# Products of 64 weight columns into two halves of PSUM, and copies of 128x1024, in a batched 64x64 matmul

## The chip, the cores and the metric

The kernel runs on one core of one Trainium2 chip. The metric is the time of one execution in microseconds on the device. Three runs of the kernel before took 133.44, 133.45 and 133.59 us, a median of 133.45. All profile lines come from one profiled execution, which is longer than its span, the stretch from the first to the last recorded event.

## The reference

There are 1024 pairs of 64x64 matrices in fp32, and each pair is multiplied:

```python
"a": np.random.randn(1024, 64, 64).astype(np.float32)
"b": np.random.randn(1024, 64, 64).astype(np.float32)
return np.matmul(a, b).astype(np.float32)
```

Each of a, b and the output is 16.78 MB, so 50.33 MB cross the HBM interface. The kernel multiplies in bf16 and accumulates in fp32.

## The kernel before, in words

The batch is cut into 16 tiles of 64 matrices (n_t, index t) for b and the output, and into 8 pairs of tiles (n_s, index s) for a. The order of work is written out by hand at the end of the function, under manual_schedule(): every engine and every DMA queue takes its instructions in the order of the calls there.

**Loads.** cast_load_a() (L73) loads three quarters of a pair's a through POOL's queue and casts to bf16 on the way; load_a() (L81) loads the last quarter as fp32 through SP's queue, into a_raw. load_first_a() (L94) loads pair 0 as fp32 into two buffers borrowed from the output pool. load_b() (L100) loads one tile of b, in turn through SP's and ACT's queues, three tiles ahead.

**Making the weights.** The contraction index is split in two (u), and two bf16 values share one fp32 word. For pairs 1 to 3 (ON_DVE), transpose_dve() transposes blocks on VectorE (L131), and ScalarE casts a_raw for it (L129). For the other pairs regroup() (L109, L112, L115) sorts the rows, and transpose() transposes on TensorE (L141) and copies the result with ScalarE (L144). spread() copies the transposed a into one of two block-diagonal weight tiles at_bd (L157 and L167, on VectorE). Four matrices (h) share the 128 rows of one weight block. cast() casts b to bf16 (L176; for the last tile L181 and L183).

**Products.** multiply(t) runs, for a tile, 16 groups g of four matrices. For every g it makes four products: two values of j, and two of u that accumulate in PSUM. Each product (L221) loads 128 weight columns and streams 64 columns of b. The 128 weight columns are wl (2) by h by mp by vo, so that wl decides the half of the 128 PSUM partitions on which a result lies. A PSUM tile o_ps holds half a tile (8 groups), 128 partitions by 1024 fp32 values, and there are two of them.

**Copies out of PSUM.** evacuate() (L209) sorts a PSUM tile into the output tile o_sb. In PSUM the partitions go by wl and the parity of g lies along the row; in o_sb the partitions go by parity and wl lies along the row. So each half needs four copies of 64 partitions by 512 values. ScalarE does them, except that VectorE does two of four in the second half of the odd tiles from 7 to 13. In the last tile the PSUM tiles are quarters, borrowed from the transposes' pool (at_ps), and two quarters are copied by ScalarE, two by VectorE, four copies of 64x256 each.

**Stores.** store(t) issues the store (L198) of a tile one iteration after it is computed (HOLD = 2), on POOL's queue as one 1 MB DMA, for tile 14 as two, and for the last tile as four on SP's and ACT's queues.

**What orders the work around the change.** In iteration t come spread(t + 1) and cast(t + 1), the loads, perhaps TensorE transposes, multiply(t) with its copies, then the preparation of later pairs, then store(t - 1). spread(t + 1) writes the weight tile that multiply(t - 1) read. ScalarE's queue holds the copies of L209, the copies of L144, the casts of L129 and half of b's loads, all in that order.

Of the kernel before, what the change touches and what calls it, by code (L numbers as in the profile page):

```python
# [8 lines left out]
fp32 = mybir.dt.float32  # L9
bf16 = mybir.dt.bfloat16  # L10
# [3 lines left out]
def kernel(  # L14
# [14 lines left out]
    nc = tc.nc  # L29
# [7 lines left out]
    N_BD = 2  # L37
    HOLD = 2
    ON_DVE = (1, 2, 3)
# [9 lines left out]
    o_pool = ctx.enter_context(tc.tile_pool(name="o_pool", bufs=8))  # L49
    t_psum = ctx.enter_context(  # L50
        tc.tile_pool(name="t_psum", bufs=4, space=bass.MemoryType.PSUM)
    )
    o_psum = ctx.enter_context(
        tc.tile_pool(name="o_psum", bufs=2, space=bass.MemoryType.PSUM)
    )

    bd_tiles = [
        consts.tile([128, 16, 4, 4, 4, 4], fp32, name=f"at_bd{i}") for i in range(N_BD)
    ]
# [5 lines left out]
    def store_queue(t, lo):  # L65
        if t < n_t - 1:
            return nc.gpsimd
        return nc.scalar if lo % 4 == 0 else nc.sync
# [15 lines left out]
    def load_first_a():  # L84

        raw = [
            o_pool.tile([128, 8, 2, 2, 64], fp32, name="o_sb")[:].rearrange(
                "p gh j wl n -> p (gh j wl n)"
            )
            for _ in range(2)  # L90
        ]
        parts = [raw[h % 2][:, 1024 * (h // 2) : 1024 * (h // 2) + 1024] for h in range(4)]
        for h in range(4):
            (nc.scalar if h % 2 else nc.sync).dma_start(out=parts[h], in_=a_v[0, h])  # L94
        a_tiles[0] = parts
# [92 lines left out]
            piece()  # L188

    def multiply(t):  # L190
        at_bd = bd_tiles[t % N_BD][:].rearrange("p g (j wl) h mp vo -> p j g (wl h mp vo)", j=2)
        at_bd = at_bd.bitcast(bf16).rearrange("p j g (c u) -> p j g c u", u=2)
        b_bf = bbf_tiles.pop(t)
        last = t == n_t - 1
        o_sb = o_pool.tile([128, 8, 2, 2, 64], fp32, name="o_sb")

        def put(lo, n):
            store_queue(t, lo).dma_start(  # L198
                out=o_v[t, :, lo : lo + n, :],
                in_=o_sb[:, lo : lo + n].rearrange("p gh j wl n -> p (gh j wl n)"),  # L200
            )

        def evacuate(o_ps, gh, n, copies):

            for par in range(2):
                for wl in range(2):
                    src = o_ps[64 * wl : 64 * wl + 64, :, par, :, :]
                    dst = o_sb[64 * par : 64 * par + 64, gh : gh + n, :, wl, :]
                    copies[2 * par + wl](dst, src)  # L209

        for half in range(2):
            if not last:
                o_ps = o_psum.tile([128, 4, 2, 2, 64], fp32, name="o_ps")
            for g8 in range(8):
                if last and g8 % 4 == 0:
                    o_ps = t_psum.tile([128, 2, 2, 2, 64], fp32, name="at_ps")
                g = 8 * half + g8
                gl = (g8 % 4 if last else g8) // 2
                for j in range(2):
                    for u in range(2):  # L220
                        nc.tensor.matmul(  # L221
                            o_ps[:, gl, g % 2, j, :],
                            at_bd[:, j, g, :, u],
                            b_bf[:, g, 64 * u : 64 * u + 64],
                            start=(u == 0),
                            stop=(u == 1),
                        )
                if last and g8 % 4 == 3:
                    copy = nc.scalar.copy if g8 == 3 else nc.vector.tensor_copy
                    evacuate(o_ps, g // 4 * 2, 2, [copy] * 4)  # L230
            if not last:
                copies = [nc.scalar.copy] * 4
                if half and t % 2 and t > 2 * max(ON_DVE):
                    copies[2:] = [nc.vector.tensor_copy] * 2
                evacuate(o_ps, 4 * half, 4, copies)
        if last:
            held[t] = [lambda q=q: put(2 * q, 2) for q in range(4)]
        else:
            whole = t < n_t - 2
            held[t] = [lambda q=q: put(q, 8 if whole else 4) for q in ([0] if whole else [0, 4])]  # L240

    with tc.manual_schedule():
        first_cast = cast_load_a(1)
        load_first_a()

        nc.vector.memset(warm[:, 0:1], 0.0)
# [15 lines left out]
        for t in range(n_t):  # L262
            s, half = t // 2, t % 2
            if t + 1 < n_t:
                spread(t + 1)
                cast(t + 1)
            if t + B_AHEAD < n_t:
                load_b(t + B_AHEAD)
            if half == 0 and 0 < s < n_s - 1 - A_AHEAD:
                load_a(s + 1 + A_AHEAD)  # L270
            if half == 0 and 0 < s < n_s - 1 and s + 1 not in ON_DVE:
                transpose(s + 1, 1)
            multiply(t)
            if t == 0:
                transpose_dve(1, 0)
                transpose_dve(1, 1)
                a_tiles.pop(1)
                load_a(A_AHEAD)
                load_a(A_AHEAD + 1)
            if t and s + 2 in ON_DVE and (half or s):  # L280
                for part in [0, 1] if t == 1 else [half]:
                    transpose_dve(s + 2, part)
                if half:
                    a_tiles.pop(s + 2)
            elif half == 0 and 0 < s and s + 2 < n_s:
                regroup(s + 2)
            elif half == 1 and s + 2 < n_s:
                transpose(s + 2, 0)
            if t >= HOLD - 1:
                store(t - HOLD + 1)  # L290
# [32 lines left out]
```

## Time and profile before

| | |
|---|---|
| median of 3 runs | 133.45 us (133.44 to 133.59) |
| profiled execution | 133.69 us |
| its span | 131.8 us |
| TensorE: matmul / weight load busy | 60.3 us (1104) / 57.2 us (1104) |
| VectorE, ScalarE, GpSimd busy | 102.0, 88.1, 33.2 us |
| HBM read and written | 33.55 and 16.78 MB, 382 GB/s over the span |
| granted TensorE clock, mean | 0.852 |

Engines: PE is TensorE's matmul and PEld its weight load, DVE is VectorE, ACT ScalarE, POOL GpSimd, SP SyncE. In the rows of slices each digit is the busy share in tenths of one of 40 equal slices. A DMA share of 1.0 means that all 16 DMA engines of the core hold a packet the whole time; it can pass 1 a little where packets overlap. The clock is the share of TensorE's full clock that was granted; up to the first record, at about 48 us, it is shown as 1.00. A matmul's own length includes its way through the array, so the distance between matmuls in a burst tells their cost, not their mean length. A queue name with a q behind an engine (ACTq, SPq) is the engine's issuing of DMAs.

### The profile page before, as it was taken

To read this page: it belongs to the slowest core of one execution; us is meant where nothing else is said; L and a number is where in the kernel's file an instruction comes from. 1 tells how busy PE (TensorE), PEld (TensorE's weight loads), DVE (VectorE), ACT (ScalarE), POOL (GpSimd) and SP (SyncE) were. 2 spreads that over 40 slices of the span, in tenths; PEclk is the share of its full clock that TensorE was granted. 3 is DMA by queue.
4 is the path that set the end of the run, shared out by engine and by line. 5 is a ranking of instruction groups with operands and counts; after the bars stand their busy time and mean duration, and the time that the engine had idled before them with its cause. 6 is when DMAs were issued, how large, how long until landed. Compare 5 with 4: busy or idle time off the path is not lost.

```text
span 131.8 us, 2749 instructions
## 1 busy us (share of the span) xinstructions
PE 60.3 (46%) x1104; PEld 57.2 (43%) x1104; DVE 102.0 (77%) x144; ACT 88.1 (67%) x158; POOL 33.2 (25%) x45
## 2 busy tenths in 40 slices
PE   0003701964090270908971983199369615366000
PEld 0003501964090270908961963198368614355000
DVE  5932099807999996999999999599999997798300
ACT  2123605599949069492999989559969998339930
POOL 6991000042016300618120204300420212041200
PEclk9999999999999998555599599559968999679755
DMA  3999999999999999999999999999999999999993
GB/s 71 344 341 306 306 306 297 270 313 319 328 316 401 347 310 308 399 390 395 314 288 364 400 397 359 306 303 389 393 390 392 395 391 393 391 405 402 402 379 135
DMA packets 18252, 44.99 MB, mean 341 GB/s; under 512 B 1088, under 2 KB 2112, under 8 KB 18240
## 3 DMA queue, kind: packets, MB, share of 16 engines
q0 software_dynamic: 7120, 21.24, 52.7%
q1 hardware_dynamic: 6064, 13.63, 28.5%
q10 hardware_dynamic: 5056, 9.96, 20.2%
q8 instruction: 8, 0.13, 0.4%
q14 instruction: 4, 0.03, 0.1%
HBM read 33.55 MB, written 16.78 MB: 382 GB/s over the span
## 4 chain that ended last, share of the span: by engine, by line
DMA 53%; ACT 16%; DVE 14%; PE 6%; issue 5%; SPq 2%; DVEq 0%; ACTq 0%
DMA b_sb<-in_b_dram 53%; ACT o_sb L209 13%; PE o_ps L221 5%; DVE at_bd L167 4%; DVE b_bf L176 4%; DVE at_bd L157 2%; ACT b_bf L176 1%; DVE at_sb L131 1%; DVE o_sb L209 1%; DVE a_bf L112 1%; SPq L94 1%; ACT a_bf L129 1%; SPq L100 1%; ACT b_bf L183 1%; DVE a_bf L115 0%
## 5 line engine op out<-in xcount | busy, mean ns | idle before, releaser
L209 ACT COPY o_sb<-o_ps 64x512 f32<-64x512 f32 x112 | 65.0, 581 | 18.5 <-PE o_ps L221 14.3
L221 PEld LDWEIGHTS <-at_bd 128*128 128x128 bf16 x1024 | 45.3, 117 | 51.5 <-DVE b_bf L176 39.6
L221 PE MATMUL o_ps<-b_bf,at_bd 128*128 128x64 bf16 x960 | 45.7, 223 | 47.1 <-DVE b_bf L176 36.8
L167 DVE COPY at_bd<-at_sb 32x1024 f32<-32x1024 f32 x40 | 29.5, 737 | 5.9 <-ACT at_sb L144 4.9
L198 POOL DMA_DIRECT2D out_dram<-o_sb x16 | 17.1, 1068 | 53.8 <-ACT at_sb L144 21.1
L157 DVE COPY at_bd<-at_sb 32x512 f32<-32x512 f32 x48 | 21.6, 451 | 1.1
L73 POOL DMA_DIRECT2D a_sb<-in_a_dram x21 | 12.0, 588 | 37.2 <-DVE at_sb L131 34.0
L176 DVE CAST b_bf<-b_sb 128x2048 bf16<-128x2048 f32 x14 | 17.4, 1245 | 4.3 <-DMA b_sb<-in_b_dram 4.0
L141 PE MATMUL at_ps<-identity,a_bf 128*128 128x128 f32 x80 | 13.3, 336 | 11.9 <-ACT a_bf L109 11.9
L141 PEld LDWEIGHTS at_ps<-identity,a_bf 128*128 128x128 f32 x80 | 12.2, 181 | 11.9 <-issue 11.9
L144 ACT COPY at_sb<-at_ps 128x512 f32<-128x512 f32 x20 | 10.8, 591 | 2.4 <-PE at_ps L141 2.0
L131 DVE STREAM_TRANSPOSE at_sb<-a_sb 128x512 f32<-128x512 f32 x9 | 8.7, 1055 | 0.0
L131 DVE STREAM_TRANSPOSE at_sb<-a_bf 128x512 f32<-128x512 f32 x3 | 3.1, 1044 | 4.6 <-ACT a_bf L129 4.6
L109 ACT CAST a_bf<-o_sb 128x1024 bf16<-128x1024 f32 x2 | 2.1, 1045 | 5.9 <-DMA o_sb<-in_a_dram 5.9
L209 DVE COPY o_sb<-o_ps 64x512 f32<-64x512 f32 x8 | 5.5, 689 | 0.2
L109 DVE CAST a_bf<-o_sb 128x1024 bf16<-128x1024 f32 x2 | 3.2, 1599 | 2.9 <-DMA o_sb<-in_a_dram 2.9
L176 ACT CAST b_bf<-b_sb 128x2048 bf16<-128x2048 f32 x1 | 1.9, 1899 | 4.5 <-DMA b_sb<-in_b_dram 4.5
L112 DVE COPY a_bf<-a_sb 128x3072 bf16<-128x3072 bf16 x4 | 4.2, 1046 | 0.0
L183 ACT CAST b_bf<-b_sb 128x512 bf16<-128x512 f32 x2 | 1.1, 614 | 4.5 <-DMA b_sb<-in_b_dram 4.5
L250 DVE MEMSET at_bd<- 128x4096 f32 x1 | 3.5, 3472 | 0.8 <-issue 0.8
L209 DVE COPY o_sb<-at_ps 64x256 f32<-64x256 f32 x8 | 3.4, 422 | 0.5 <-PE at_ps L221 0.4
L129 ACT CAST a_bf<-a_raw 128x1024 bf16<-128x1024 f32 x3 | 3.1, 1045 | 0.1
(16 smaller groups left out, 15.4 us busy)
## 6 DMA issues: line engine op xcount, KB each, us to landing
out_dram<-o_sb POOLq DMA_DIRECT2D x14, 1024.0 KB, 21.5
a_sb<-in_a_dram POOLq DMA_DIRECT2D x21, 256.0 KB, 14.2
a_raw<-in_a_dram SPq DMA_DIRECT2D x7, 512.0 KB, 17.5
o_sb<-in_a_dram SPq DMA_DIRECT2D x2, 512.0 KB, 6.8
o_sb<-in_a_dram ACTq DMA_DIRECT2D x2, 512.0 KB, 7.5
out_dram<-o_sb POOLq DMA_DIRECT2D x2, 512.0 KB, 5.9
out_dram<-o_sb SPq DMA_DIRECT2D x2, 256.0 KB, 4.6
out_dram<-o_sb ACTq DMA_DIRECT2D x2, 256.0 KB, 4.6
```

What stands on the lines that cost most here:

```text
L73: nc.gpsimd.dma_start(out=a_sb[:, h, :, :].rearrange("p v k -> p (v k)"), in_=a_v[s, h], single_packet=True)
L109: copy(a_bf[:, :, h, :], a_sb[h].rearrange("p (v k) -> p v k", v=16))
L112: nc.vector.tensor_copy(a_bf[:, :, 0:3, :], cast_sb[:].rearrange("p h v k -> p v h k"))
L131: nc.vector.transpose(at_tiles[s][:, h].rearrange("p g w mp vo -> p w vo g mp"), pairs.rearrange("p (vo w kp) -> p w vo kp", vo=4, w=4),)
L141: nc.tensor.transpose(at_ps[:, vo, :], a_cols[:, 4 * vo + 2 * j + wl, :], identity[:])
L144: nc.scalar.copy(at_tiles[s][:, :, 2 * j + wl, :, :], at_ps[:].rearrange("p vo (g mp) -> p g mp vo", mp=4),)
L157: nc.vector.tensor_copy(bd[rows, 8 * i : 8 * i + 8, :, h, :, :].rearrange("p g w mp vo -> p (g w) (mp vo)"), at_sb[block : block + 32, h]. ...
L167: nc.vector.tensor_copy(bd[rows, :, :, h, :, :].rearrange("p g w mp vo -> p (g w) (mp vo)"), at_sb[rows, half].rearrange("p g w mp vo -> p ...
L176: (nc.vector.tensor_copy if t else nc.scalar.copy)(b_bf[:], b_sb[:])
L198: store_queue(t, lo).dma_start(out=o_v[t, :, lo : lo + n, :], in_=o_sb[:, lo : lo + n].rearrange("p gh j wl n -> p (gh j wl n)"),)
L209: copies[2 * par + wl](dst, src)
L221: nc.tensor.matmul(o_ps[:, gl, g % 2, j, :], at_bd[:, j, g, :, u], b_bf[:, g, 64 * u : 64 * u + 64], start=(u == 0), stop=(u == 1),)
```

## The change

The PSUM partitions now go by the parity of the group, as they do in o_sb. A product uses 64 weight columns (h, mp, vo for one w of four) and writes 64 partitions: groups with even g the lower half, odd ones the upper half. Within a PSUM tile, the two parities alternate, product by product. So there are 128 products and 128 weight loads per tile instead of 64, each again with 64 streamed columns of b. PSUM then has the order of o_sb, and one copy of 128 partitions by 1024 values empties a PSUM tile. ScalarE makes all of these copies; VectorE has none left except two of 128x512 for the last tile, of which ScalarE copies the other two quarters. The number and order of loads, casts, spreads, transposes and stores are the same.

```diff
     def multiply(t):
-        at_bd = bd_tiles[t % N_BD][:].rearrange("p g (j wl) h mp vo -> p j g (wl h mp vo)", j=2)
-        at_bd = at_bd.bitcast(bf16).rearrange("p j g (c u) -> p j g c u", u=2)
+        at_bd = bd_tiles[t % N_BD][:].rearrange("p g w h mp vo -> p w g (h mp vo)")
+        at_bd = at_bd.bitcast(bf16).rearrange("p w g (c u) -> p w g c u", u=2)
...
-        def evacuate(o_ps, gh, n, copies):
-
-            for par in range(2):
-                for wl in range(2):
-                    src = o_ps[64 * wl : 64 * wl + 64, :, par, :, :]
-                    dst = o_sb[64 * par : 64 * par + 64, gh : gh + n, :, wl, :]
-                    copies[2 * par + wl](dst, src)
...
-            for g8 in range(8):
-                if last and g8 % 4 == 0:
-                    o_ps = t_psum.tile([128, 2, 2, 2, 64], fp32, name="at_ps")
-                g = 8 * half + g8
-                gl = (g8 % 4 if last else g8) // 2
-                for j in range(2):
+                o_ps = o_psum.tile([128, 4, 4, 64], fp32, name="o_ps")
+            for q in range(4):
+                if last and q % 2 == 0:
+                    o_ps = t_psum.tile([128, 2, 4, 64], fp32, name="at_ps")
+                gl = q % 2 if last else q
+                for w in range(4):
                     for u in range(2):
-                        nc.tensor.matmul(
-                            o_ps[:, gl, g % 2, j, :],
-                            at_bd[:, j, g, :, u],
-                            b_bf[:, g, 64 * u : 64 * u + 64],
-                            start=(u == 0),
-                            stop=(u == 1),
-                        )
-                if last and g8 % 4 == 3:
-                    copy = nc.scalar.copy if g8 == 3 else nc.vector.tensor_copy
-                    evacuate(o_ps, g // 4 * 2, 2, [copy] * 4)
+                        for par in range(2):
+                            g = 8 * half + 2 * q + par
+                            nc.tensor.matmul(
+                                o_ps[64 * par : 64 * par + 64, gl, w, :],
+                                at_bd[:, w, g, :, u],
+                                b_bf[:, g, 64 * u : 64 * u + 64],
+                                start=(u == 0),
+                                stop=(u == 1),
+                            )
+                if last and q % 2:
+                    copy = nc.scalar.copy if q == 1 else nc.vector.tensor_copy
+                    gh = 4 * half + q - 1
+                    copy(o_sb[:, gh : gh + 2], o_ps[:])
             if not last:
-                copies = [nc.scalar.copy] * 4
-                if half and t % 2 and t > 2 * max(ON_DVE):
-                    copies[2:] = [nc.vector.tensor_copy] * 2
-                evacuate(o_ps, 4 * half, 4, copies)
+                nc.scalar.copy(o_sb[:, 4 * half : 4 * half + 4], o_ps[:])
```

The output tile is now declared as [128, 8, 4, 64], the same memory as [128, 8, 2, 2, 64] before.

More of the change, by code (lines that the diff above doesn't have):

```diff
@@ L86, in load_first_a @@
         raw = [
-            o_pool.tile([128, 8, 2, 2, 64], fp32, name="o_sb")[:].rearrange(
-                "p gh j wl n -> p (gh j wl n)"
+            o_pool.tile([128, 8, 4, 64], fp32, name="o_sb")[:].rearrange(
+                "p gh w n -> p (gh w n)"
             )
@@ L190, in multiply @@
     def multiply(t):
-        at_bd = bd_tiles[t % N_BD][:].rearrange("p g (j wl) h mp vo -> p j g (wl h mp vo)", j=2)
-        at_bd = at_bd.bitcast(bf16).rearrange("p j g (c u) -> p j g c u", u=2)
+        at_bd = bd_tiles[t % N_BD][:].rearrange("p g w h mp vo -> p w g (h mp vo)")
+        at_bd = at_bd.bitcast(bf16).rearrange("p w g (c u) -> p w g c u", u=2)
         b_bf = bbf_tiles.pop(t)
         last = t == n_t - 1
-        o_sb = o_pool.tile([128, 8, 2, 2, 64], fp32, name="o_sb")
+        o_sb = o_pool.tile([128, 8, 4, 64], fp32, name="o_sb")
         def put(lo, n):
@@ L199, in put @@
                 out=o_v[t, :, lo : lo + n, :],
-                in_=o_sb[:, lo : lo + n].rearrange("p gh j wl n -> p (gh j wl n)"),
+                in_=o_sb[:, lo : lo + n].rearrange("p gh w n -> p (gh w n)"),
             )
-        def evacuate(o_ps, gh, n, copies):
-            for par in range(2):
-                for wl in range(2):
-                    src = o_ps[64 * wl : 64 * wl + 64, :, par, :, :]
-                    dst = o_sb[64 * par : 64 * par + 64, gh : gh + n, :, wl, :]
-                    copies[2 * par + wl](dst, src)
@@ L211, in multiply @@
         for half in range(2):
             if not last:
-                o_ps = o_psum.tile([128, 4, 2, 2, 64], fp32, name="o_ps")
-            for g8 in range(8):
-                if last and g8 % 4 == 0:
-                    o_ps = t_psum.tile([128, 2, 2, 2, 64], fp32, name="at_ps")
-                g = 8 * half + g8
-                gl = (g8 % 4 if last else g8) // 2
-                for j in range(2):
-                    for u in range(2):
-                        nc.tensor.matmul(
-                            o_ps[:, gl, g % 2, j, :],
-                            at_bd[:, j, g, :, u],
-                            b_bf[:, g, 64 * u : 64 * u + 64],
-                            start=(u == 0),
-                            stop=(u == 1),
-                        )
-                if last and g8 % 4 == 3:
-                    copy = nc.scalar.copy if g8 == 3 else nc.vector.tensor_copy
-                    evacuate(o_ps, g // 4 * 2, 2, [copy] * 4)
+                o_ps = o_psum.tile([128, 4, 4, 64], fp32, name="o_ps")
```

## The prediction

> **What bounds the kernel now.** I read the page's slices and queues first, then the stretches of the last microseconds, then the groups, then TensorE and ScalarE in order of time.
>
> ```profile
> DMA  3999999999999999999999999999999999999993
> q8 instruction: 8, 0.13, 0.4%
> HBM read 33.55 MB, written 16.78 MB: 382 GB/s over the span
> DMA 53%; ACT 16%; DVE 14%; PE 6%; issue 5%; SPq 2%; DVEq 0%; ACTq 0%
> ```
>
> The 16 DMA engines are busy in every slice but the first and the last. The chain that ended last spends over half of its length in loads of b. Stretches of the span (PE, PEld, DVE, ACT, POOL busy, then clock, DMA share, GB/s):
>
> ```profile
> 70.00:80.00 10.00, 7.26 (x139) 6.95 (x140) 9.71 (x14) 9.27 (x18) 1.27 (x2) 0.83 1.03 395
> 118.00:120.00 2.00, 1.37 (x47) 1.37 (x48) 1.56 (x4) 1.95 (x5) 0.00 (x0) 1.00 1.05 412
> 128.00:129.00 1.00, 0.00 (x0) 0.00 (x0) 0.00 (x0) 0.00 (x0) 0.00 (x0) 0.50 0.95 338
> 129.00:130.00 1.00, 0.00 (x0) 0.00 (x0) 0.00 (x0) 0.00 (x0) 0.00 (x0) 0.50 0.70 246
> 130.00:131.00 1.00, 0.00 (x0) 0.00 (x0) 0.00 (x0) 0.00 (x0) 0.00 (x0) 0.50 0.09 31
> ```
>
> In the middle VectorE (9.71 of 10) and ScalarE (9.27) look like the limit, but the DMA share is 1.03 beside them, and it stays at 0.95 or more until 129.0, 2.5 us after the last compute instruction (126.5). All 50.33 MB at the 395 to 412 GB/s of these rows take 122.2 to 127.4 us, of a span of 131.8. The transfers are the bound; the engines keep just ahead of them. Groups (busy, mean ns of one | idle before):
>
> ```profile
> L209 ACT COPY o_sb<-o_ps 64x512 f32<-64x512 f32 x112 | 65.0, 581 | 18.5 <-PE o_ps L221 14.3
> L221 PEld LDWEIGHTS <-at_bd 128*128 128x128 bf16 x1024 | 45.3, 117 | 51.5 <-DVE b_bf L176 39.6
> L221 PE MATMUL o_ps<-b_bf,at_bd 128*128 128x64 bf16 x960 | 45.7, 223 | 47.1 <-DVE b_bf L176 36.8
> L141 PEld LDWEIGHTS at_ps<-identity,a_bf 128*128 128x128 f32 x80 | 12.2, 181 | 11.9 <-issue 11.9
> L144 ACT COPY at_sb<-at_ps 128x512 f32<-128x512 f32 x20 | 10.8, 591 | 2.4 <-PE at_ps L141 2.0
> L129 ACT CAST a_bf<-a_raw 128x1024 bf16<-128x1024 f32 x3 | 3.1, 1045 | 0.1
> ```
>
> A ScalarE copy goes by its length, not its partitions (64x512: 581 ns, 128x512: 591). TensorE and ScalarE in order of time (start, length):
>
> ```profile
> 45.25 3.49 PE L221 MATMUL o_ps<-b_bf,at_bd 128*128 128x64 bf16 x64 [5.57 <-DVE b_bf L176]
> 77.72 1.11 PE L221 MATMUL o_ps<-b_bf,at_bd 128*128 128x64 bf16 x32 [0.38 <-ACT at_sb L144]
> 118.63 2.04 PE L221 MATMUL at_ps<-b_bf,at_bd 128*128 128x64 bf16 x64 [1.31 <-DVE at_bd L167]
> 118.73 4.74 ACT L209 COPY o_sb<-o_ps 64x512 f32<-64x512 f32 x8
> 126.55 0.38 ACTq L198 DMA_DIRECT2D out_dram<-o_sb  x1
> ```
>
> One product with its weight load costs 3.49/64 = 54 ns at the low clock and 1.11/32 = 35 ns at the full one. So a tile's 64 products take 3.5 or 2.2 us, far below the 5.8 us from one tile to the next (starts 96.73, 102.58, 108.39).
>
> **The copies.** Removed on ScalarE: 112 x 581 ns = 65.0 us, and 8 of 64x256 at 367 ns (2.9 us). Added: 30 of 128x1024, bounded by the 1045 ns of that shape from SBUF and by 2 x 591 = 1182 ns (two 128x512 from PSUM); I take 1.05, the same shape, so 31.5 us, and 2 x 0.59 for the last tile. ScalarE loses about 35 us of its 88. VectorE loses its 8 copies of 689 ns (5.5 us), and at the end 8 x 422 ns = 3.4 become two of 128x512, each between 689 (64x512) and 844 (2 x 422); 0.7 taken, 2.0 us saved. None of this is counted: the full DMA queues hide it. If that cover were gone, it would show where VectorE sets the pace; it waits for b in only 4.0 us of the whole run, so the compute side alone might gain up to its 5.5 us.
>
> **The products.** 1024 products of 128 weight columns become 2048 of 64, and loads likewise; each still streams 64 columns of b. Lower bound of one: half of today's, if the two halves of the array run side by side (27 or 17 ns). Upper: load and stream one after the other, 2 x 54 or 2 x 35 = 108 or 70 ns. I take today's pace, 54 or 35 ns, because the trace shows loads under streams: in the transposes (L141), where a load of 128 f32 columns has 181 ns and sixteen pairs take 3.65 us from 11.90 (228 each), matmul and load busy times overlap (13.3 and 12.2 us for 80). A tile then takes 128 x 54 = 6.9 us cold, or 128 x 35 = 4.5 us at the full clock; with 8 transposes (1.95/16 = 0.12 us each in the burst from 99.93) 5.5 us, still under 5.8. TensorE stays hidden by the transfers when it is at the full clock; cold it is not (second rival).
>
> [...]
>
> **What is queued behind a longer tile.** Tile 0 starts at 22.66; its results would leave ScalarE at 22.66 + 6.9 + 1.05 = 30.6 instead of 29.31, and the cast of a_raw (L129, at 29.33) stands behind them, 1.3 us later (1.7 us earlier if the halves run side by side). VectorE's transpose waits for that (idle 4.59 us there), as do SP's next load of a_raw and the load of b behind it (issued 31.39, landed 51.42). With 20.0 us of queue in front of that load, the engines of the DMA do not run dry; VectorE had 1.03 us of waiting to spare at 51.44. Counted: nothing for the end, at most 0.3 us left over for the compute side. The new waits are the same semaphore as before (a copy on its half's products, spread() on the tile before last); POOL's stores only drop their wait on VectorE.
>
> **The end.** Tile 14's copies shrink from 4.74 to 2.1 us. The last tile's products run from 118.63 to 123.1 at the full clock, its last VectorE copy to 123.8, so the last store is issued about 2.7 us before today's 126.55. That buys nothing as long as the DMA is full: shares 0.95, 0.70 and 0.09 after 128 leave 0.05 + 0.30 = 0.35 us idle on average before 130, 0.4 to 0.5 with the full level at 1.03 to 1.05. This is all that an even finish could win.
>
> **The instruction transfers.** TensorE's instructions go from 2208 (1104 + 1104 in the page) to 4256. Queue q8 moves 0.13 MB in 8 packets, 0.4% of 16 engines: 0.53 us of each engine on average, or 16 x 0.53/8 = 1.05 us of one engine for one packet. If they are TensorE's, 8 more come. Bounds at the end: 0 (they fall on engines that finish early) and 1.05 us (one falls on the last engine); below nothing they can't go, since they add work. I take 0.4, near the mean of 0.53 less a part that the uneven finish swallows.
>
> [...]
>
> **Sum.** The profiled execution took 133.69 us, a span of 131.8 and 1.9 around it. 0 for copies, 0 for products, 0 for the earlier stores, +0.4 for instructions: 134.1 against 133.69. The median of the runs is 133.45, 0.24 lower, so 133.45 + 0.4 = 133.85.
>
> **Rivals.** First, faster: the stores of the last two tiles are ready 2.7 us sooner, engines that end early take up the new packets, and the uneven finish (0.4 to 0.5 us) closes. It decides if the extra packets cost the last engine under 0.1 us. Time 133.45 - 0.4 = 133.0. For it: shares of 0.70 and 0.09 at the end. Against it: the DMA is already full to 129.
>
> Second, TensorE late: from 77 to 118 us it must follow a period of 5.8 us, and the clock there alternates (0.66 to 1.00 by stretch). A cold tile with 8 transposes (0.23 each) takes 6.9 + 1.8 = 8.7 us, 2.9 more than the period; a warm one takes up only 0.3. Three cold tiles of eight lose 8.7 and win back 1.5, less the 2.7 us of the earlier end and the 2.5 us in which the DMA outlasts compute today: +2.0. Time 134.5 to 137. For it: bursts at 54 ns up to 52 us and again at 85.09 (3.59 us). Against: a busier TensorE had the higher clock here (1.00 from 100 to 110).
>
> [...]
>
> Fourth, loads not hidden: 108 or 70 ns a product. TensorE then works without pause from 22.66: 16 x 128 x 70 ns = 143 us and 64 transposes 7.8, so 22.7 + 143 + 7.8 = 174, with the tail about 180; if the true warm price is the stream alone twice (2 x 29, as the 1.11 us less the 0.19 us length of the last product give), about 155. For it: nothing here shows 64-column loads. Against: loads overlap streams in both of today's kinds.
>
> That the halves run side by side changes none of these sums but the second: it lowers its chance.
>
> **How the numbers follow.** The DMA decides as before, with the new packets: 0.60, time 133.3 to 134.5, predicted 133.85. Faster: 0.13. TensorE late: 0.14. Loads at a fixed pace: 0.04. Loads exposed: 0.09. A measurement tells about 0.2% from no change, 0.27 us: up to 133.72 counts as same. Of the first case's 0.60 I give 0.21 to same and 0.39 to slower. So faster 0.13, same 0.21, slower 0.39 + 0.14 + 0.04 + 0.09 = 0.66. The range leaves out the last two cases (0.13) and the far end of the late case and of the faster one: 132.9 to 136.5.
>
> **What would show it.** Right: DMA share at 1.0 through to 129, ScalarE near 53 us busy, 16 packets on q8, 30 ScalarE copies near 1.05 us, tiles of 128 products in 4 to 7 us, the end of compute near 124 and the span 131.9 to 132.9. Wrong: stretches with a DMA share under 0.9 before 125; VectorE's spread() or b casts waiting for products; TensorE busy without a gap; or a DMA that moves more than 412 GB/s.

## The result, and the profile after

The changed kernel takes 134.84 us (134.72 to 134.96) against 133.44 us for the kernel before, measured beside it: ratio 1.0103, 95% interval 1.0085 to 1.0120. It is 1.4 us slower. The profiled execution took 134.72 us with a span of 132.9, that of before 133.69 and 131.8: 1.0 and 1.1 us more.

The page of the changed kernel: busy share of the DMA engines by slice, the instruction queue, and the chain that ended last.

```profile
DMA  3999999999999999999999999999999999999984
q8 instruction: 16, 0.26, 0.7%
DMA 57%; DVE 16%; PE 10%; issue 8%; ACT 3%; SPq 2%; DVEq 0%
```

The DMA is full until near the end, as before; q8, the queue that carries instructions, has 16 packets instead of 8. ScalarE's share of the chain has fallen from 16% to 3%, and the time did not follow. The groups (busy, mean ns of one | idle before, and its releaser):

```profile
L214 PEld LDWEIGHTS <-at_bd 128*64 128x64 bf16 x2048 | 49.3, 141 | 55.1 <-DVE b_bf L176 31.0
L214 PE MATMUL o_ps<-b_bf,at_bd 128*64 128x64 bf16 x1920 | 48.5, 225 | 49.6 <-DVE b_bf L176 29.3
L226 ACT COPY o_sb<-o_ps 128x1024 f32<-128x1024 f32 x30 | 30.2, 1016 | 43.4 <-PE o_ps L214 43.4
```

Twice the products and loads take about the busy time of before (48.5 and 49.3 us, against 45.7 and 45.3). ScalarE's copies take 30.2 us instead of 65.0. TensorE in order of time:

```profile
60.68 3.62 PE L214 MATMUL o_ps<-b_bf,at_bd 128*64 128x64 bf16 x128 [3.89 <-DVE b_bf L176]
...
66.89 2.49 PE L214 MATMUL o_ps<-b_bf,at_bd 128*64 128x64 bf16 x128 [0.22 <-DVE b_bf L176]
...
99.64 2.83 PE L214 MATMUL o_ps<-b_bf,at_bd 128*64 128x64 bf16 x98 [2.33 <-issue]
...
105.84 2.02 PE L214 MATMUL o_ps<-b_bf,at_bd 128*64 128x64 bf16 x114 [0.96 <-issue]
109.92 0.41 PE L214 MATMUL o_ps<-b_bf,at_bd 128*64 128x64 bf16 x14 [2.06 <-DVE b_bf L176]
112.03 2.99 PE L214 MATMUL o_ps<-b_bf,at_bd 128*64 128x64 bf16 x128 [1.70 <-issue]
118.23 3.25 PE L214 MATMUL o_ps<-b_bf,at_bd 128*64 128x64 bf16 x114 [3.21 <-issue]
121.24 0.61 PE L214 MATMUL at_ps<-b_bf,at_bd 128*64 128x64 bf16 x14
124.15 3.01 PE L214 MATMUL at_ps<-b_bf,at_bd 128*64 128x64 bf16 x114 [2.30 <-issue]
```

128 products take 3.62 us at the low clock (granted 0.50; 28 ns each) and 2.49 at the full one (granted 1.00; 19.5 ns). That is near the lower bound of the forecast (27 and 17 ns), which has two halves of the array side by side, but no run puts all products into one half, so it is not told apart here from the loads of 64 columns instead of 128 (in the records those last longer, 141 ns on average against 117). New are long waits in the middle of a tile that nothing in the profile releases ("issue"): TensorE stops 14 products into tiles 14 and 15. Its restarts at 99.64, 105.84, 112.03, 118.23 and 124.15 are 5.9 to 6.2 us apart, and between two of them lie 256 TensorE instructions, 128 products or transposes with their loads. A packet of q8 (16 KB, 0.26 MB in 16) starts 2.3 to 2.5 us before each restart. This points to a TensorE that waits for its own instructions; the experiments test it. The end, by stretches (PE, PEld, DVE, ACT, POOL busy, then clock, DMA share, GB/s):

```profile
124.00:126.00 2.00, 1.85 (x71) 1.85 (x72) 0.27 (x1) 0.58 (x1) 0.00 (x0) 0.50 0.99 383
126.00:127.00 1.00, 1.00 (x53) 1.00 (x47) 0.42 (x1) 0.41 (x1) 0.00 (x0) 0.66 0.65 250
127.00:128.00 1.00, 0.17 (x11) 0.05 (x3) 0.69 (x1) 0.17 (x1) 0.00 (x0) 1.00 0.84 307
...
130.00:131.00 1.00, 0.00 (x0) 0.00 (x0) 0.00 (x0) 0.00 (x0) 0.00 (x0) 0.55 0.77 268
131.00:132.00 1.00, 0.00 (x0) 0.00 (x0) 0.00 (x0) 0.00 (x0) 0.00 (x0) 0.50 0.20 71
```

The last products end at 127.2, so the stores of the last tile come late, and the DMA runs partly dry from 126 to 128 (0.65, 0.84). It works on until 131.6, where it ended at 130.4 before (0.09 in 130 to 131 there). The two readings that suggest themselves are the dry stretch, and the longer tail of the DMA. The experiments tell them apart.

### The profile page after: what moved, and what is told of

It reads as the page before. It is cut to its first block, busy times and chain, and to the rows that moved or that the text cites. A ratio compares the mean times of both kernels' runs of the same rounds, so it can differ in the third digit from the quotient of the medians.

```text
span 132.9 us, 4676 instructions
## 1 busy us (share of the span) xinstructions
PE 63.6 (48%) x2128; PEld 60.2 (45%) x2128; DVE 94.1 (71%) x130; ACT 51.2 (39%) x70; POOL 33.6 (25%) x45
## 4 chain that ended last, share of the span: by engine, by line
DMA 57%; DVE 16%; PE 10%; issue 8%; ACT 3%; SPq 2%; DVEq 0%
DMA b_sb<-in_b_dram 57%; PE o_ps L214 8%; DVE at_bd L157 7%; DVE b_bf L176 6%; PE at_ps L214 3%; DVE at_sb L131 1%; ACT b_bf L176 1%; SPq L94 1%; ACT o_sb L226 1%; ACT a_bf L129 1%; DVE a_bf L112 1%; SPq L100 1%; DVE o_sb L224 1%; DVE a_bf L115 0%; SPq L81 0%
## 5 line engine op out<-in xcount | busy, mean ns | idle before, releaser
L214 PEld LDWEIGHTS <-at_bd 128*64 128x64 bf16 x2048 | 49.3, 141 | 55.1 <-DVE b_bf L176 31.0
L214 PE MATMUL o_ps<-b_bf,at_bd 128*64 128x64 bf16 x1920 | 48.5, 225 | 49.6 <-DVE b_bf L176 29.3
L226 ACT COPY o_sb<-o_ps 128x1024 f32<-128x1024 f32 x30 | 30.2, 1016 | 43.4 <-PE o_ps L214 43.4
L167 DVE COPY at_bd<-at_sb 32x1024 f32<-32x1024 f32 x40 | 28.5, 712 | 6.4 <-ACT at_sb L144 5.0
L198 POOL DMA_DIRECT2D out_dram<-o_sb x16 | 16.8, 1050 | 47.6 <-ACT o_sb L226 40.2
L73 POOL DMA_DIRECT2D a_sb<-in_a_dram x21 | 12.8, 627 | 42.1 <-DVE at_sb L131 37.1
L141 PE MATMUL at_ps<-identity,a_bf 128*128 128x128 f32 x80 | 12.2, 316 | 11.6 <-ACT a_bf L109 11.6
L141 PEld LDWEIGHTS at_ps<-identity,a_bf 128*128 128x128 f32 x80 | 10.8, 166 | 11.8 <-issue 11.6
L224 DVE COPY o_sb<-at_ps 128x512 f32<-128x512 f32 x2 | 1.4, 692 | 7.3 <-PE at_ps L214 7.3
L214 PE MATMUL at_ps<-b_bf,at_bd 128*64 128x64 bf16 x128 | 3.6, 234 | 2.3 <-issue 2.3
L115 DVE CAST a_bf<-a_raw 128x1024 bf16<-128x1024 f32 x4 | 3.1, 775 | 0.0
```

Source lines behind the costliest of these rows:

```text
L73: nc.gpsimd.dma_start(out=a_sb[:, h, :, :].rearrange("p v k -> p (v k)"), in_=a_v[s, h], single_packet=True)
L141: nc.tensor.transpose(at_ps[:, vo, :], a_cols[:, 4 * vo + 2 * j + wl, :], identity[:])
L167: nc.vector.tensor_copy(bd[rows, :, :, h, :, :].rearrange("p g w mp vo -> p (g w) (mp vo)"), at_sb[rows, half].rearrange("p g w mp vo -> p ...
L198: store_queue(t, lo).dma_start(out=o_v[t, :, lo : lo + n, :], in_=o_sb[:, lo : lo + n].rearrange("p gh w n -> p (gh w n)"),)
L214: nc.tensor.matmul(o_ps[64 * par : 64 * par + 64, gl, w, :], at_bd[:, w, g, :, u], b_bf[:, g, 64 * u : 64 * u + 64], start=(u == 0), stop= ...
L226: nc.scalar.copy(o_sb[:, 4 * half : 4 * half + 4], o_ps[:])
```

## The experiments

Ratios are to the kernel before, run on the same chip beside each set; its median there was 133.48 to 133.61 us.

**The two parts of the change, each alone.** First the copies with the old products:

```diff
...
             if not last:
-                copies = [nc.scalar.copy] * 4
-                if half and t % 2 and t > 2 * max(ON_DVE):
-                    copies[2:] = [nc.vector.tensor_copy] * 2
-                evacuate(o_ps, 4 * half, 4, copies)
+                nc.scalar.copy(o_sb[:, 4 * half : 4 * half + 4], o_ps[:])
```

> Products as before (64 per tile, 128 weight columns), copies as changed (one of 128x1024 per half tile); since PSUM is then in the old order, results land in permuted places of the output, the work is otherwise the same. Refill theory (TensorE runs out of instructions, because 256 of them must come through the full DMA engines and that takes about 6 us): instructions stay at 2208, no wait before 64-product bursts but for b and the weights, time 133.2 to 133.6, as before. Rival, the wide copies cost the time (their reads or writes slow VectorE, which then is late): about 134.8.

Measured: 133.79 us, ratio 1.0012 (1.0003 to 1.0022). ScalarE's 88 us of work became 50.5 and VectorE's 102 became 93.5, and nothing was gained. Then the products with the old copies (four 64x512 per half tile, split between ScalarE and VectorE as before):

```diff
...
-                nc.scalar.copy(o_sb[:, 4 * half : 4 * half + 4], o_ps[:])
...
+                evacuate(o_ps, 4 * half, 4, copies)
```

> Products as changed (128 per tile, 64 weight columns), copies of 64x512 as before, 8 a tile, VectorE with its share in the odd tiles from 7 to 13. Refill theory: 16 packets on q8, TensorE waits of 2 to 3.5 us with no releaser, 134.6 to 136, since the longer copies now follow a TensorE that is late. Rival, wide copies: 133.4.

Measured: 134.98 us, ratio 1.0103 (1.0088 to 1.0118), with the waits. Its row in the table of waits (who for whom: us in total, times, longest):

```profile
PEld L221 <- issue: 17.8, 15, 3.4
```

The longest, 3.4 us, is a pause ahead of the first products that the kernel before has too (its row says 5.0 us in all, three times). The whole loss belongs to the products. The wide copies bring nothing; their ratio lies just above 1, by 0.2 us. This run does not tell transfers from waits: its last copy ends at 129.5, and its DMA share is still 1.02 from 130 to 131.

**The number of TensorE's instructions or the kind of product.**

```diff
-                    for u in range(2):
+                    for u in range(1):
                         for par in range(2):
...
-                                stop=(u == 1),
+                                stop=True,
```

> The changed kernel without the second of the two accumulating products (u = 1 is left out): half of the contraction is missing from the output. 64 products of 64 weight columns per tile, 2208 TensorE instructions again, copies as changed. Refill theory: 8 packets on q8, no waits without releaser in the last 60 us, DMA share near 1 to 129, time 133.0 to 133.6. Rival, products into one half of the array are slow in themselves or drain: a tile still takes over half of 3.6 us, and the time stays above 134. Rival, wide copies: 134.8.

Measured: 133.72 us, ratio 1.0007 (0.9997 to 1.0016). So products into one half of PSUM did not cost the time by their kind, 64 of them a tile, and neither did their loads. The end of its TensorE, in order of time:

```profile
108.61 1.92 PE L214 MATMUL o_ps<-b_bf,at_bd 128*64 128x64 bf16 x64 [4.46 <-DVE b_bf L176]
113.93 1.92 PE L214 MATMUL o_ps<-b_bf,at_bd 128*64 128x64 bf16 x64 [3.40 <-DVE b_bf L176]
117.55 1.92 PE L214 MATMUL at_ps<-b_bf,at_bd 128*64 128x64 bf16 x64 [1.70 <-ACT b_bf L183]
```

Every one of these bursts waits for data again, none for instructions. The opposite, many instructions with products of the old kind:

```diff
                 for j in range(2):
-                    for u in range(2):
+                    for u in (0, 1, 0, 1):
                         nc.tensor.matmul(
```

> The kernel before with every product issued twice (the second pair starts the sum again, so the result is the same): 128 products of 128 weight columns per tile, 4256 TensorE instructions, copies as before. Refill theory: the waits without releaser come back, one per 128 products about 6 us apart, time 134.8 to 137 (the copies are longer than in the changed kernel, and a product costs 54 or 29 ns instead of 28 or 20). Rival, the 64-column products are what costs: no such waits, 133.4 to 134.0, with 0.5 us for 8 more packets.

Measured: 138.47 us, ratio 1.0353 (1.0325 to 1.0381), above what was expected. Waits without releaser are back (11.3 and 4.6 us in its table), and here TensorE is late in earnest, with 3.9 us for 128 products even at the full clock (granted 1.00 from 126 to 130; 30 ns each) and long copies behind it. The DMA runs dry:

```profile
122.00:124.00 2.00, 1.75 (x62) 1.66 (x59) 1.92 (x4) 1.76 (x4) 0.66 (x1) 1.00 0.40 154
124.00:126.00 2.00, 0.99 (x35) 0.87 (x32) 1.91 (x4) 1.95 (x4) 0.69 (x1) 1.00 0.38 133
```

This is what a late TensorE looks like when it sets the time: the DMA share falls to 0.40 and 0.38. It does not divide the changed kernel's 1.4 us.

**The dry stretch or the transfers.** Tiles 14 and 15 go back to the old products and copies. multiply_128() is the old multiply(), added to the changed kernel:

```diff
...
-            multiply(t)
+            (multiply_128 if t >= n_t - 2 else multiply)(t)
```

> The changed kernel, but tiles 14 and 15 with products and copies as before. If the loss is 0.5 us of DMA time for instructions plus about 0.6 us in which the DMA runs dry at the end, because tiles 14 and 15 wait for instructions: no DMA share under 0.9 before 129, 14 or 15 packets on q8, 133.7 to 134.2. If the whole loss is the transfers of instructions: 134.6 to 134.8. If the dry stretch is the whole loss: 133.4.

Measured: 134.85 us, ratio 1.0095 (1.0077 to 1.0113). The end of the DMA in this kernel:

```profile
126.00:127.00 1.00, 0.00 (x0) 0.00 (x0) 0.00 (x0) 0.98 (x3) 0.00 (x0) 0.94 1.02 370
127.00:128.00 1.00, 0.00 (x0) 0.00 (x0) 0.00 (x0) 0.08 (x1) 0.00 (x0) 0.50 1.04 374
128.00:129.00 1.00, 0.00 (x0) 0.00 (x0) 0.00 (x0) 0.00 (x0) 0.00 (x0) 0.50 1.03 366
129.00:130.00 1.00, 0.00 (x0) 0.00 (x0) 0.00 (x0) 0.00 (x0) 0.00 (x0) 0.50 0.84 314
130.00:131.00 1.00, 0.00 (x0) 0.00 (x0) 0.00 (x0) 0.00 (x0) 0.00 (x0) 0.50 0.47 166
131.00:132.00 1.00, 0.00 (x0) 0.00 (x0) 0.00 (x0) 0.00 (x0) 0.00 (x0) 0.50 0.15 53
```

The dry stretch from 126 to 128 is gone, and the time is the same. My theory that the waits of the last two tiles cost some 0.6 us fell here. Of the three outcomes on record, the one in which the whole loss is the transfers of instructions came, just above its 134.8. With half of the tiles changed:

```diff
...
-            multiply(t)
+            (multiply_128 if t % 2 else multiply)(t)
```

> Even tiles as changed, odd tiles as before: 192 products for two tiles, so 256 instructions last about 1.3 tiles, over 7 us at 5.8 us a tile. Refill theory: waits without releaser nearly vanish, 12 packets on q8, and only half of the 0.5 us of added transfers is left: 133.4 to 133.9. Rival, the 64-column products or the wide copies cost the time by their number: half of the loss, about 134.1.

Measured: 134.78 us, ratio 1.0087 (1.0067 to 1.0106), another miss: half the added packets (12 instead of 16) cost nearly the whole loss, although the waits without releaser are nearly gone (4.3 us in all, of which 3.5 are one pause ahead of the first products that the kernel before has too). So the loss is not proportional to the packets. That led to the last theory, a guess, as the trace does not name the engine of a packet: the packets of q8 go round over 8 of the 16 DMA engines, so that 8 packets give one to each, 9 to 16 give some engine two, and the engine that ends last sets the time.

**The step.** Three kernels count it out: the kernel before with tiles 2 and 3 changed (9 packets), the changed kernel with one tile's products issued twice (17), and the kernel before with half of its products left out (4).

```diff
...
-            multiply(t)
+            (multiply if t in (2, 3) else multiply_128)(t)
```

> The kernel before, with only tiles 2 and 3 as changed: 2464 TensorE instructions, so 9 packets on q8 instead of 8, and no new wait for instructions in the last 60 us. Step theory (the packets of q8 go round over 8 of the 16 DMA engines, each holds its engine for 1.0 us, and the time is set by the last engine, so the ninth packet falls on an engine that already has one): up to 1.0 us more, 134.2 to 134.6 where the kernel before has 133.5. Rival, the loss follows the added bytes evenly: 0.06 us, no difference. Rival, the loss is TensorE's waits for instructions near the end: no difference.

Measured: 134.89 us, ratio 1.0110 (1.0097 to 1.0124). One packet more, and the whole loss is there, more than the 1.0 us that was the most expected. Its waits without releaser are those of the kernel before (5.0 us in all, three times, 3.5 the longest), so here the loss comes without any new wait of TensorE. Instruction queue (from the page), then the end of its DMA:

```profile
q8 instruction: 9, 0.15, 0.4%
```

```profile
128.00:129.00 1.00, 0.00 (x0) 0.00 (x0) 0.00 (x0) 0.00 (x0) 0.00 (x0) 0.50 1.01 356
129.00:130.00 1.00, 0.00 (x0) 0.00 (x0) 0.00 (x0) 0.00 (x0) 0.00 (x0) 0.50 0.77 271
130.00:131.00 1.00, 0.00 (x0) 0.00 (x0) 0.00 (x0) 0.00 (x0) 0.00 (x0) 0.50 0.16 53
131.00:132.00 1.00, 0.00 (x0) 0.00 (x0) 0.00 (x0) 0.00 (x0) 0.00 (x0) 0.50 0.04 13
```

A share of 0.04 of 16 engines for 1 us is 0.6 us of a single engine: about what one engine that works on alone past 131 would leave. The same stretch has 0.15 in the kernel with 12 packets (2.4 engine-us, 0.6 for each of four) and 0.20 in the changed one with 16 (3.2, 0.4 for each of eight). The stretch ahead of it gives an estimate of the number of late engines. From 130.6 to 131.0 the shares are 0.07 with 9 packets, 0.27 with 12, 0.47 with 15 and 0.57 with 16, which is 1.1, 4.3, 7.5 and 9.1 engines on average, where the theory has one, four, seven and eight with a second packet; in these traces a full DMA counts as up to 1.08 (10 to 30 us of the kernel before). In the kernel before all has ended by then.

```diff
-                    for u in range(2):
+                    for u in (0, 1, 0, 1) if t == 2 else (0, 1):
```

> The changed kernel with the products of tile 2 issued twice (the sum starts again, so the result is the same): 4512 TensorE instructions, 17 packets on q8, and the places at which later tiles wait for instructions stay the same, since exactly 256 are added. Step theory: a third packet on one engine, up to 1.0 us above the changed kernel's 134.84, so 135.3 to 135.9. Rival, even spread of bytes: 134.9. Rival, waits near the end: 134.8 to 134.9.

Measured: 135.96 us, ratio 1.0189 (1.0176 to 1.0202), 1.1 us above the changed kernel and just above the 135.9 that was the most expected.

```profile
q8 instruction: 17, 0.28, 0.8%
```

```profile
130.00:131.00 1.00, 0.00 (x0) 0.00 (x0) 0.00 (x0) 0.00 (x0) 0.00 (x0) 0.50 0.68 239
131.00:132.00 1.00, 0.00 (x0) 0.00 (x0) 0.00 (x0) 0.00 (x0) 0.00 (x0) 0.50 0.30 107
132.00:133.00 1.00, 0.00 (x0) 0.00 (x0) 0.00 (x0) 0.00 (x0) 0.00 (x0) 0.50 0.05 18
```

Again the time of about a single engine is left, 0.05 of 16 or 0.8 us, this time past 132.

```diff
-                    for u in range(2):
+                    for u in range(1):
                         nc.tensor.matmul(
...
-                            stop=(u == 1),
+                            stop=True,
```

> The kernel before without the second of the two accumulating products (u = 1 is left out, half of the contraction is missing from the output): 1184 TensorE instructions, 4 packets on q8 instead of 8, otherwise the same. Step theory: four engines still have one packet each, so the last engine ends as before: no difference from 133.5 (within 0.15). Rival, even spread of bytes: 0.25 us less. If TensorE's waits near the end matter in the kernel before: also less, by up to 0.5 us.

Measured: 133.47 us, ratio 1.0003 (0.9991 to 1.0015): no difference, as expected of a step. Its DMA share from 129.6 to 130.0 is 0.35, against 0.61 in the kernel before: four packets fewer, and about four engines (4.2) fewer work on at the end, but the last of them ends no earlier. In a table, without the run with doubled products (16 packets, 138.47 us) and the one with small stores below, whose DMA is not full:

| packets on q8 | kernels | us |
|---|---|---|
| 4 | before, half the products | 133.47 |
| 8 | before; wide copies; half of the new products | 133.44 to 133.61; 133.79; 133.72 |
| 9 | tiles 2 and 3 changed | 134.89 |
| 12 | even tiles changed | 134.78 |
| 15 | all but tiles 14 and 15 changed | 134.85 |
| 16 | changed; new products with old copies | 134.84; 134.98 |
| 17 | changed, one tile twice | 135.96 |

**What a refill is made of.**

```diff
-            held[t] = [lambda q=q: put(q, 8 if whole else 4) for q in ([0] if whole else [0, 4])]
+            held[t] = [lambda q=q: put(q, 1 if whole else 4) for q in ([0] if whole else [0, 4])]
```

> The changed kernel with stores of one eighth of tiles 0 to 13 (seven eighths of their output is left out), 12.8 MB less, about 32 us of DMA time. The question is what the 6 us of a refill is made of. If TensorE's instructions queue behind data in the full DMA engines: once the DMA is not full, the wait before TensorE's bursts without releaser falls well under 2 us, and refills follow each other faster than 6 us where the products do. If it is a fixed latency: the waits of 2 to 3.5 us stay.

One run: 123.45 us, with most of the output left out, and inconclusive on the question. From about 86 us on, the DMA is no longer full, and TensorE in order of time shows both:

```profile
96.40 2.83 PE L214 MATMUL o_ps<-b_bf,at_bd 128*64 128x64 bf16 x98 [3.97 <-issue]
99.16 2.84 PE L141 MATMUL at_ps<-identity,a_bf 128*128 128x128 f32 x16
101.93 4.58 PE L214 MATMUL o_ps<-b_bf,at_bd 128*64 128x64 bf16 x256
108.45 0.42 PE L214 MATMUL o_ps<-b_bf,at_bd 128*64 128x64 bf16 x14 [1.93 <-DVE b_bf L176]
109.23 1.99 PE L214 MATMUL o_ps<-b_bf,at_bd 128*64 128x64 bf16 x114 [0.37 <-issue]
```

256 products run without a break, and some waits shrink to 0.37 us. But there is still one of 3.97 us, and the start of a packet still lies 2.3 us or more ahead of the restart. Packets of q8 can follow each other 3.6 to 4.6 us apart here, against 6.0 to 6.4 under a full DMA (the changed kernel from 72 to 122 us), which suggests that part of the refill is queueing and part is not. How large each part is stays open.

No kernel of these that stores the whole output beats the kernel before. With 8 packets or fewer, wide copies and lighter engines end at the same 133.5 to 133.8 us: the DMA, whose share from 128 to 129 is still 0.95 or 0.96 in three of the four, is read here as what sets it.

## Why the prediction was right or wrong

The prediction of slower and the range held; the size did not: +0.4 us was forecast, +1.4 measured between the medians and +1.0 between the profiled executions. That the range held is luck in part: 134.84 lies above the 133.3 to 134.5 of my own case and inside the 134.5 to 137 of the rival with a late TensorE, whose cause, cold tiles longer than 5.8 us, did not come: they took 3.6. The term that was mis-sized is that of the instruction transfers. It had the right count (8 more packets, 16 from 4256 instructions), with bounds of 0 and 1.05 us. I took 0.4, near the mean over 16 engines, though the note beside the upper bound said when it holds: when a packet falls on the last engine. By the step theory the engine that ends last sets the end of a full DMA, and the ninth packet falls on an engine that already has one. The runs give 1.1 to 1.4 us per step, so even the upper bound was short. A packet of q8 takes 0.9 to 1.1 us in these traces; what the rest of the step is stays open. In every run the number of packets is that of the full groups of 256 in TensorE's instructions: 4, 8, 9, 12, 15, 16 and 17 packets for 1184, 2208, 2464, 3232, 4000, 4256 and 4512 instructions.

One reading ahead of the sum was wrong, without harm to it. The 395 to 412 GB/s of the rows count 44.99 MB in all (the page's DMA packets line), since the 21 loads of a that cast on the way stand there with 256 KB each in bf16, half of what they read. So the 50.33 MB cannot be divided by these rates. That the transfers set the time rests on the DMA share and on the runs with lighter engines.

Point by point:

- **Copies hidden: right.** 1016 ns each against about 1050 taken, ScalarE 51.2 us busy against about 53, VectorE 94.1 instead of 102.0. The run with wide copies alone shows that nothing of it reaches the time.
- **Products hidden: right in effect, wrong in the pace.** 28 and 19.5 ns, near the lower bound (27 and 17), not 54 and 35. 128 loads and products took 2.49 us at the full clock. The rival with exposed loads (108 or 70 ns a product) fell. Loads at a fixed pace, which had a chance of 0.04, are shown by no run: the products followed the clock, from 28 to 19.5 ns.
- **The queue behind tile 0: the time of the case with halves side by side.** The cast of a_raw came at 26.88 instead of 29.33, 2.4 us earlier, where I had 1.7. The terms of that sum (22.66 + 128 x 0.027 + 1.05) give 2.1, and the products began 0.35 us earlier.
- **The end of compute: wrong.** I had the last VectorE copy end at 123.8; it ended at 127.9. The list of what TensorE waits for lacked its own instructions: 3.2 us in tile 14 and 2.3 us in tile 15. The rival of a late TensorE came in its place for another reason than the clock, and the kernel with the last two tiles put back shows that it cost no time.
- **The earlier stores buy nothing: right in effect**, though they never came earlier, and the share of 1.0 until 129 failed between 126 and 128.
- **The faster rival: fell** at its own condition, that the extra packets cost the last engine under 0.1 us.

What is shown is the step between 8 and 9 and between 16 and 17 packets, its absence from 4 to 8 and its near absence from 9 to 16, and a DMA tail worth about one, four, seven and nine engines (1.1, 4.3, 7.5 and 9.1). That the packets go round over eight engines in a fixed order is inferred from this; the trace does not name the engines, and no kernel has fewer than 4 packets.

## What to carry to other kernels

When the DMA is full from start to end, count everything that uses it, instructions too, and ask what falls on the engine that ends last rather than on the average one. Here a change that took 36.9 us of work from ScalarE and 7.9 from VectorE but doubled TensorE's products and loads lost 1.4 us, and one packet too many (9 instead of 8) cost as much as eight. Before trusting a suspicious stretch, such as a DMA running dry near the end, take it away and see whether the time moves.

## What the runs showed of the hardware that was not expected

- With the DMA share at about 1.0, TensorE's restarts were 5.9 to 6.2 us apart, with 256 of its instructions between two of them, while 128 products with their loads took 2.5 to 3.6 us, and single waits lasted up to 3.5 us (the run with 17 packets).
- Each packet of instructions (16 KB) took 0.9 to 1.1 us, and the time moved in steps while the DMA was full: 133.4 to 133.8 us with 4 or 8 packets, 134.8 to 135.0 with 9 to 16, 135.96 with 17.
- Products of 64 weight columns that alternate between the halves of the PSUM partitions ran at 28 ns each at the low clock (0.50) and 19.5 ns at the full one (1.00), loads included, against 54 and 30 to 35 ns for products of 128 columns.
